# Block transposes and 128-byte DMAs in place of TensorE transposes, a thread per RWKV end, and a pause between narrow visits

## The chip, the core and the metric

The kernel runs on one core of one Trainium2 chip. The metric is the device time of one execution in microseconds (us); several executions are timed and their median is taken. One more execution is profiled. The engines are TensorE (PE; its weight loads PEld), VectorE (DVE), ScalarE (ACT), GpSimd (POOL) and SyncE (SP). SP computes nothing here: it issues DMAs, one after the other, in the order in which the program names them.

## What is computed

One layer of an encoder over 512 frames of 2048 features, in float32. A projection of x feeds two mixers: 16 RWKV-7 heads of 64 and 8 HGRN2 heads of 128. Their gated outputs are concatenated, projected back and added to x ahead of a LayerNorm.

```python
proj = einsum('btd,dc->btc', h, w_in)
rw, hg = token_shift(proj[..., :RWKV_COLS], mu), proj[..., RWKV_COLS:]
# RWKV-7, per frame and head:
S = S * w_t + (S @ a_t) b_t^T + v_t k_t^T ;  o_t = S @ r_t
o = group_norm(o) * gn_w + gn_b + sum(r * k * r_k) * v ;  o_rwkv = o * silu(z)
# HGRN2, chunk by chunk of 64 frames:
o = o_intra + (q * exp(b)) @ S ;  S = S * exp(b_last) + k_dec^T @ i
o_hgrn = o * rsqrt(mean(o*o) + eps) * g_norm_w * silu(z)
h = layer_norm(ALPHA * h + concat(o_rwkv, o_hgrn) @ w_out)
```

## The kernel before, in words

Features lie on the 128 partitions and the 512 frames along them, so a tile is 128x512. Each float32 product of the two large projections is made as three products of reduced-precision halves (`three`, L441): activations `xh`, `xl`, weights `wh`, `wl`. SP loads weights in tiles `wr` of 128x1024 (`load`, L420; two buffers); of each half of a `wr`, a *part*, ACT makes `wh` (L330) and DVE `wl` (`split`, L405; L340). A part feeds 12 main products of 128x128 by 128x512 on TensorE (L446). There are three buffers each of `wh` and `wl`. A `wr` buffer is loaded again once both of its parts are split.

Everything else runs beside these main products, in threads: `rwkv_prep` (one per pair of RWKV heads), `rwkv_invert` and `rwkv_scan` (one per group of two pairs), `rwkv_finish` (the end of a pair), `hgrn_heads` with `hgrn_out` (two heads together, then each head's keys, states and end), and `put_gated`, which stores most gated outputs to HBM until the output projection asks for them. A thread is a generator that yields one instruction or one condition at a time.

`Plan` (L63) writes the program while it is built: it keeps an estimated clock per engine, and after every main product it asks the first thread of each queue (`pump`, L194; `step`, L158) whether its next instruction could start about now. What it takes is written at that place of that engine's queue. So the order of each engine is fixed when the kernel is built; on the chip each engine goes through its own queue in order and waits by semaphores. TensorE's instructions have three modes: *main* (reduced precision, 512 wide), *whole* (f32, 128x128 and all rows) and *narrow* (f32, fewer rows or columns). `TURNS` prices a change of mode, and `worth` (L183) holds a visit back for a moment so that others can join.

Two ways of turning a tile are in the kernel. `tr` (L320) is a TensorE transpose of 128x128 against the identity, into PSUM (L321). `turned` (L385) is the other: DVE transposes each 32x32 block in place in its tile (`dtr`, L358; L359), then 16 DMAs (8 with `rows=2`) on SP's queue carry each row of blocks to its partitions, in pieces of 32 floats, 128 bytes (L394). The planner writes the DMAs in four groups, lets its clock go on by 0.4 us for each DMA of a group, and counts the tile as there 3 us after the last group. Before, `rwkv_prep` turns two tiles per pair so: `bk`, 128x1024, in 16 DMAs, and the values `v` into `zz`, in 8.

The other turns are TensorE's. `rwkv_finish` (L890) transposes four blocks of `o_all` into the PSUM tile `po`, and DVE (L349) multiplies and adds from it into `g`. `hgrn_out` transposes three blocks of keys `k` into `ps`, copied to `kt` (inside the tile `g`) for TensorE's state products, and at its end four blocks of `o2` into `pn`, which DVE multiplies into `g`. All ends of RWKV pairs wait in a single queue, `finishes`, of which only the first thread is asked.

Of the kernel before, what the change touches and what calls it, by code (L numbers as in the profile page):

```python
# [62 lines left out]
class Plan:  # L63
# [8 lines left out]
    TURNS = {("main", "whole"): 0.015, ("whole", "main"): 0.033, ("main", "narrow"): 0.1,  # L72
             ("whole", "narrow"): 0.1, ("narrow", "main"): 0.26, ("narrow", "whole"): 0.2}
    LEAD = -0.35
    SLACK = 0.6
    EARLY = 0.5

    def __init__(self, room):
        self.clock = {"pe": 0.0, "dve": 0.0, "act": 0.0, "pool": 0.0, "dma": 0.0}
        self.table = None  # L80
        self.mode = "main"
# [43 lines left out]
    def issue(self, op, way=None):  # L125
        end, s, r, e, f = way or self.best(op)
        f()
        if e == "pe":
            self.mode = op.mode
        if op.table and self.table not in op.table:  # L130
            self.table = op.table[0]
# [103 lines left out]
def mixer_kernel(ctx, tc, head, x_r, w_all, par, up, ln_wb, consts, hmask, out):  # L235
# [149 lines left out]
    def turned(dst, src, tmp, rows=4, base=0):  # L385
# [5 lines left out]
        for a in range(4):  # L391
            for b in range(rows):
                o = base + 32 * b
                nc.sync.dma_start(dst[o : o + 32, :, 32 * a : 32 * a + 32],  # L394
                                  tmp[32 * a : 32 * a + 32, :, 32 * b : 32 * b + 32])
            at = plan.clock["pe"] + 0.4 * rows
            yield lambda: plan.clock["pe"] >= at
# [492 lines left out]
    def rwkv_finish(S, p):  # L890
# [26 lines left out]
        drop(po)  # L917
        yield stt(z, sz, 1.0, z, ALU.add, ALU.mult)
# [4 lines left out]
    def rwkv_group(SS, grp):  # L923
# [126 lines left out]
    def hgrn_out(S, h, q, k, dt_, dg, tot, tots):  # L1050
# [3 lines left out]
        kt, state = tiles(g)[:, 0:3], tiles(k)[:, 0:3]  # L1054
        yield landed(k)
        ps = take("mix")
        for t in range(3):
            yield tr(ps[:, t * P : t * P + P], k[:, t * P : t * P + P])
        yield copy(kt, tiles(ps)[:, 0:3])
        drop(ps)  # L1060
        yield has(S, "i")
# [26 lines left out]
        S["used"]()  # L1088
        yield landed(o2)
        pn = take("mix")  # L1090
        for j in range(4):
            yield tr(pn[:, j * P : j * P + P], o2[:, j * P : j * P + P])
        yield has(S, "g")
        yield stt(g, pn, hcol(HHW, h), S["g"], ALU.mult, ALU.mult)
        drop(S["g"], pn, o2)
        put_gated(8 + h, g)
# [563 lines left out]
```

## Time and profile before

| | us |
|---|---|
| timed runs, median of 3 | 1053.51 (1051.52 to 1053.82) |
| the profiled execution's own time | 1053.89 |
| its span, first to last instruction | 1052.1 |
| PE busy | 1042.6 (99%) |
| DVE busy | 755.1 (72%) |
| ACT busy | 438.0 (42%) |
| transposes on PE (L321) | 88 |
| DMAs of turned tiles on SP (L394) | 128 of 256 pieces into `q`, 64 into `zz` |
| mean granted TensorE clock | 0.998 |

How to read it: a group of instructions is named by its line, engine, operation, and output<-inputs with the buffer numbers left out. Matmuls overlap, so the step from one start to the next tells more than a length. A f32 matmul that isn't a transpose stands twice in the trace, as two passes. The timeline's columns are start, length, engine and group; the chain of work in order of time has the same without shapes.

### The profile page before, as it was taken

The page shows a single profiled execution, that of the slowest core. Times are in us where ns is not written, and L with a number is a line of the kernel's source. Part 1 is how long each engine was busy: PE and PEld are TensorE (multiplying, and loading weights), DVE is VectorE, ACT ScalarE, POOL GpSimd, SP SyncE. Part 2 cuts the span into 40 slices and gives each one's busy share as a digit, 9 for nine tenths or more (in the row PEclk, how much of TensorE's full clock was granted, in tenths as well). Part 3 has the DMA queues.
Part 4 walks back from the last instruction along what each step waited for, and adds up shares of the span by engine and source line. Part 5 has one row for each costly group of instructions (what it writes and reads, how often), then busy time and mean ns, then how long its engine had stood idle before and what let it go on. Part 6 is the DMA issues. An engine that isn't in the chain of part 4 may idle for free.

```text
span 1052.1 us, 18837 instructions
## 1 busy us (share of the span) xinstructions
PE 1042.6 (99%) x7342; PEld 867.6 (82%) x7342; DVE 755.1 (72%) x1653; ACT 438.0 (42%) x867; POOL 37.4 (4%) x81
## 2 busy tenths in 40 slices
PE   9999999999999999999999999999999999999997
PEld 8888888888888888888888888888888788888885
DVE  7475898667769987676688856865998677725556
ACT  6445243444352344552533344525235454323321
POOL 0000000000000000000000000000000001000000
PEclk9999999999999999999999999999999999999999
DMA  8134343222343522223534223234352143545613
GB/s 332 51 104 113 98 112 86 85 79 80 84 123 101 122 80 85 73 91 80 137 83 123 88 66 100 69 91 122 96 125 70 58 166 126 186 128 158 203 61 130
DMA packets 87305, 114.79 MB, mean 109 GB/s; under 512 B 56368, under 2 KB 58160, under 8 KB 87088
## 3 DMA queue, kind: packets, MB, share of 16 engines
q1 hardware_dynamic: 87072, 113.39, 36.5%
q8 instruction: 58, 0.95, 0.4%
q14 instruction: 31, 0.25, 0.1%
q10 hardware_dynamic: 144, 0.20, 0.1%
HBM read 99.92 MB, written 7.34 MB: 102 GB/s over the span
## 4 chain that ended last, share of the span: by engine, by line
PE 99%; DVE 1%; issue 0%; DVEq 0%
PE main L446 74%; PE mix L317 11%; PE mix L446 8%; PE main L1185 3%; PE main L317 2%; PE mix L321 1%; PE mix L1135 0%; DVE inv L349 0%; DVE inv L340 0%; DVE stats L1542 0%; DVEq L1656 0%; DVE mv L1350 0%; DVE mv L345 0%; DVE inv L1133 0%; DVE mv L349 0%
## 5 line engine op out<-in xcount | busy, mean ns | idle before, releaser
L446 PE MATMUL main<-xh,wl 128*128 128x512 f32 x864 | 342.4, 396 | 0.0
L446 PE MATMUL main<-xh,wh 128*128 128x512 f32 x864 | 341.6, 395 | 0.0
L446 PE MATMUL main<-xl,wh 128*128 128x512 f32 x864 | 340.9, 395 | 0.0
L330 ACT ACTIVATE wh<-wr 128x512 fp32r<-128x512 f32 x299 | 186.8, 626 | 234.9 <-PE main L446 167.2
L340 DVE TENSOR_TENSOR wl<-wr,wh 128x512 fp32r<-128x512 f32 x299 | 203.7, 682 | 61.2 <-ACT wh L330 59.7
L446 PEld LDWEIGHTS main<-xh,wl 128*128 128x128 f32 x864 | 162.7, 188 | 33.0
L446 PEld LDWEIGHTS main<-xl,wh 128*128 128x128 f32 x864 | 162.7, 188 | 32.8
L446 PEld LDWEIGHTS main<-xh,wh 128*128 128x128 f32 x864 | 162.8, 188 | 32.6
L446 PE MATMUL main<-wh,xh 128*128 128x512 f32 (+1 forms) x262 | 102.4, 391 | 0.0
L446 PE MATMUL main<-wh,xl 128*128 128x512 f32 (+1 forms) x262 | 102.1, 390 | 0.0
L446 PE MATMUL main<-wl,xh 128*128 128x512 f32 (+1 forms) x262 | 102.1, 390 | 0.0
L446 PEld LDWEIGHTS main<-wl,xh 128*128 128x128 f32 x262 | 49.2, 188 | 9.8
L446 PEld LDWEIGHTS main<-wh,xl 128*128 128x128 f32 x262 | 49.2, 188 | 9.7
L446 PEld LDWEIGHTS main<-wh,xh 128*128 128x128 f32 x262 | 49.2, 188 | 9.5
L331 ACT ACTIVATE t<-main,om 128x512 f32<-128x512 f32 x33 | 22.4, 687 | 53.5 <-PE main L446 42.3
L349 DVE SCALAR_TENSOR_TENSOR t<-main,pr,t 128x511 f32<-128x511 f32 x33 | 24.4, 747 | 28.1 <-ACT t L331 27.7
L340 DVE TENSOR_TENSOR inv<-inv,inv 64x30 f32<-64x30 f32 (+14 forms) x120 | 38.6, 322 | 2.9
L340 DVE TENSOR_TENSOR inv<-inv 64x30 f32<-64x30 f32 (+14 forms) x120 | 38.4, 320 | 2.3
L340 DVE TENSOR_TENSOR t<-t,tot 128x256 f32<-128x256 f32 x96 | 37.9, 415 | 1.9 <-PE mix L317 1.7
L349 DVE SCALAR_TENSOR_TENSOR bd<-mix,pc,bd 64x64 f32<-64x64 f32 x112 | 31.7, 283 | 9.5 <-PE mix L317 7.2
L330 ACT ACTIVATE zz<-mix 64x64 f32<-64x64 f32 x61 | 13.4, 219 | 45.6 <-PE mix L317 43.9
L331 ACT ACTIVATE t<-main 128x512 f32<-128x512 f32 x32 | 18.5, 598 | 30.6 <-PE main L446 30.2
(222 smaller groups left out, 1331.2 us busy)
## 6 DMA issues: line engine op xcount, KB each, us to landing
wr<-w_all SPq DMA_DIRECT2D x156, 512.0 KB, 3.6
q<-head SPq DMA_DIRECT2D x15, 448.0 KB, 5.5
q<-q SPq DMA_DIRECT2D x128, 32.0 KB, 2.4
g<-x_r SPq DMA_DIRECT2D x16, 256.0 KB, 4.0
spill<-g SPq DMA_DIRECT2D x12, 256.0 KB, 2.8
out<-q SPq DMA_DIRECT2D x12, 256.0 KB, 2.4
t<-spill SPq DMA_DIRECT2D x10, 256.0 KB, 4.0
zz<-ksq SPq DMA_DIRECT2D x64, 32.0 KB, 2.7
```

The lines of the kernel that those rows point to most:

```text
L317: return Op([("pe", cost, lambda: pe.matmul(o, l, r, start=start, stop=stop, **kw))], [l, r], [o], mode="narrow" if narrow else "main" if ...
L321: return Op([("pe", 0.11, lambda: pe.transpose(o, i, ident))], [i], [o])
L330: return "act", cost, lambda: sc_e.activation(o, i, f, scale=scale)
L331: return "act", cost, lambda: sc_e.activation(o, i, f, scale=scale, bias=bias)
L340: return dve_op([a, b], o, lambda: dve.tensor_tensor(o, a, b, f), base=0.16 if o.shape[0] < P and size(o) == C and o.tensor.name in tags e ...
L349: return dve_op([a, b], o, lambda: dve.scalar_tensor_tensor(o, a, s, b, f1, f2), per=0.00113, base=0.085 if o.shape[0] == P else 0.25 if s ...
L446: pe.matmul(ps, l, r, start=first and i == 0, stop=last and i == 2)
L1185: pe.matmul(pss[a], *ops, start=k == 0 and low == of == 0, stop=k == KT - 1 and low == 1)
```

## The change

- Six of the eight RWKV ends (pairs 0 to 5) turn `o_all` by `turned`, through a `ksq` buffer: a block transpose on DVE and 16 DMAs of 32x4x32 on SP. DVE's multiply-add then reads the tile in SBUF itself.
- In HGRN heads 0 to 5 the keys are turned so (16 DMAs of 32x3x32, straight into `kt`), and the end too (16 DMAs of 32x4x32, in place).
- `turned` lets the planner's clock go on by 0.2 us per DMA and not 0.4, for all tiles, `bk` and `zz` too.
- `finishes` becomes two queues, one for each pair of a group.
- After a narrow visit, `worth` lets none begin from another mode for 1.5 us of the planner's clock.

```diff
+    REST = 1.5
...
         if e == "pe":
             self.mode = op.mode
+            if op.mode == "narrow":
+                self.rest = end + self.REST
...
     def worth(self, op, now):
+        if op.mode == "narrow" != self.mode and now < self.rest:
+            return False
...
-            at = plan.clock["pe"] + 0.4 * rows
+            at = plan.clock["pe"] + 0.2 * rows
...
-        drop(sm, sq)
+        drop(sm)
+        if p < 6:
+            yield from turned(o_all, o_all, tiles(sq.rearrange("p a b -> p (a b)")))
+        drop(sq)
...
-        yield landed(o_all)
-        po = take("mix")
-        for j in range(4):
-            yield tr(po[:, j * P : j * P + P], o_all[:, j])
+        if p < 6:
+            po = o_all.rearrange("p j f -> p (j f)")
+        else:
+            yield landed(o_all)
+            po = take("mix")
+            for j in range(4):
+                yield tr(po[:, j * P : j * P + P], o_all[:, j])
...
-                plan.add(finishes, rwkv_finish(S, 2 * grp + i))
+                plan.add(finishes[i], rwkv_finish(S, 2 * grp + i))
...
+        if h < 6:
+            yield room(ksq=1)
+            tmp = take("ksq")
+            yield from turned(kt, tiles(k)[:, 0:3], tiles(tmp)[:, 0:3])
+            drop(tmp)
+        else:
+            yield landed(k)
+            ps = take("mix")
...
+        if h < 6:
+            yield room(ksq=1)
+            tmp = take("ksq")
+            yield from turned(tiles(o2), tiles(o2), tiles(tmp))
+            drop(tmp)
+            pn = o2
+        else:
+            yield landed(o2)
+            pn = take("mix")
...
-    groups, finishes, preps = plan.queue(), plan.queue(), plan.queue()
+    groups, finishes, preps = plan.queue(), [plan.queue(), plan.queue()], plan.queue()
```

The planner writes nearly every queue anew. Rows of the orders below give line, operation, output<-inputs with buffer numbers, shape and count; lines after the change are those of the changed file (L401 there is L394 before, L347 is L340, L356 is L349, L366 is L359, L324 is L317, L453 is L446).

**Place A**, after the scan of the first group. SP before: `q4374` is the `bk` tile of pair 2, `g481` the gated output of pair 0.

```order
L394 DMA q4374_2307<-q4468_2805 32x8x32 x8
L423 DMA wr480_2881<-w_all 128x1024
L394 DMA q4374_2307<-q4468_2805 32x8x32 x8
L423 DMA wr490_2938<-w_all 128x1024
L599 DMA spill_109<-g481_2885 128x512
L423 DMA wr497_2983<-w_all 128x1024
L423 DMA wr507_3029<-w_all 128x1024
L394 DMA zz501_3005<-ksq502_3006 32x8x32 x8
```

SP now: `q4369` is that `bk`, `t141` and `t204` are the ends of pairs 0 and 1.

```order
L401 DMA q4369_2302<-q4482_2931 32x8x32 x16
L430 DMA wr494_3025<-w_all 128x1024
L401 DMA t141_677<-ksq471_2881 32x4x32 x12
L401 DMA t204_1006<-ksq473_2883 32x4x32 x4
L401 DMA t141_677<-ksq471_2881 32x4x32 x4
L401 DMA t204_1006<-ksq473_2883 32x4x32 x8
L430 DMA wr501_3091<-w_all 128x1024
L401 DMA t204_1006<-ksq473_2883 32x4x32 x4
L430 DMA wr510_3140<-w_all 128x1024
L606 DMA spill_109<-g497_3074 128x512
L401 DMA zz512_3150<-ksq513_3151 32x8x32 x8
```

Before, loads stood between the halves of one turn; now three turns, 48 DMAs, stand with two loads among them.

DVE at place A before, from the block transpose of `bk` to the multiply-add of pair 0's end, which reads PSUM (`mix483`):

```order
L359 STREAM_TRANSPOSE q4468_2805<-q4374_2307 128x1024
L340 TENSOR_TENSOR wl472_2828<-wr447_2674,wh471_2827 128x512
L349 SCALAR_TENSOR_TENSOR t475_2841<-main448_2682,pr_104,t475_2841 128x511
L353 TENSOR_REDUCE sm461_2775<-ksq462_2776 128x8
L340 TENSOR_TENSOR wl477_2855<-wr460_2734,wh476_2854 128x512
L346 TENSOR_SCALAR sm461_2775<-sm461_2775 128x8
L340 TENSOR_TENSOR wl479_2877<-wr460_2734,wh478_2876 128x512
L340 TENSOR_TENSOR t141_677<-t141_677,sm461_2775 128x512
L349 SCALAR_TENSOR_TENSOR g481_2885<-mix483_2898,half_106,t106_460 128x512
L340 TENSOR_TENSOR wl485_2913<-wr473_2836,wh484_2912 128x512
```

DVE now, from the block transpose of pair 0's end on; `ksq507` is a half that a TensorE product of pair 3's preparation reads.

```order
L366 STREAM_TRANSPOSE ksq471_2881<-t141_677 128x512
L347 TENSOR_TENSOR t204_1006<-t204_1006,sm472_2882 128x512
L347 TENSOR_TENSOR wl493_3021<-wr481_2919,wh492_3020 128x512
L366 STREAM_TRANSPOSE ksq473_2883<-t204_1006 128x512
L347 TENSOR_TENSOR wl496_3052<-wr488_2975,wh495_3051 128x512
L347 TENSOR_TENSOR wl500_3087<-wr488_2975,wh499_3086 128x512
L356 SCALAR_TENSOR_TENSOR g497_3074<-t141_677,half_106,t106_460 128x512
L356 SCALAR_TENSOR_TENSOR t503_3104<-main487_2972,pr_104,t503_3104 128x511
L356 SCALAR_TENSOR_TENSOR t463_2814<-ksq498_3075,t463_2814 128x512
L347 TENSOR_TENSOR wl505_3115<-wr494_3025,wh504_3114 128x512
L356 SCALAR_TENSOR_TENSOR g497_3074<-g497_3074,half_106,t463_2814 128x512
L347 TENSOR_TENSOR ksq507_3126<-t425_2590,ksq506_3125 128x512
```

The multiply-add `g497<-t141` now reads the tile that the DMAs write, and the splits `wl505` and `ksq507` stand behind it. The block transpose of `bk` (`q4482`) stands five rows ahead of the first of these, with the split `wl486` right behind it.

TensorE at place A before: the four transposes of pair 0's end.

```order
L446 MATMUL main474_2839<-xl26_93,wh476_2854 128x512
L446 MATMUL main474_2839<-xh10_77,wl477_2855 128x512
L321 MATMUL mix483_2898<-cst_100,t141_677 128x128 x4
L446 MATMUL main474_2839<-xh11_78,wh476_2854 128x512
L446 MATMUL main474_2839<-xl27_94,wh476_2854 128x512
```

TensorE now: they are gone; the product that reads `ksq507` stands here, 59 products of 512 columns behind the first one of `wl486`'s part, and `wl505`'s part begins two rows further on.

```order
L453 MATMUL main502_3102<-xh8_75,wh499_3086 128x512
L324 MATMUL mix511_3146<-ksq506_3125,ones_r_102 128x512
L324 MATMUL mix511_3146<-ksq507_3126,ones_r_102 128x512
L453 MATMUL main502_3102<-xl24_91,wh499_3086 128x512
L453 MATMUL main502_3102<-xh8_75,wl500_3087 128x512
L453 MATMUL main502_3102<-xh9_76,wh504_3114 128x512
L453 MATMUL main502_3102<-xl25_92,wh504_3114 128x512
L453 MATMUL main502_3102<-xh9_76,wl505_3115 128x512
```

**Place B**, after the scan of the second group. SP before, around the `bk` of pair 4 (`q4668`):

```order
L394 DMA q4668_4116<-q4811_5022 32x8x32 x8
L423 DMA wr821_5082<-w_all 128x1024
L394 DMA q4668_4116<-q4811_5022 32x8x32 x8
L423 DMA wr831_5141<-w_all 128x1024
L599 DMA spill_109<-g822_5089 128x512
L423 DMA wr838_5184<-w_all 128x1024
L394 DMA zz844_5211<-ksq845_5212 32x8x32 x2
L423 DMA wr848_5232<-w_all 128x1024
L394 DMA zz844_5211<-ksq845_5212 32x8x32 x6
```

SP now: `t428` and `t555` are the ends of pairs 2 and 3, `q4651` and `zz840` pair 4's, `t599` the end of head 3.

```order
L401 DMA t428_2617<-ksq797_5063 32x4x32 x4
L401 DMA t555_3363<-ksq799_5065 32x4x32 x4
L430 DMA wr824_5249<-w_all 128x1024
L401 DMA t555_3363<-ksq799_5065 32x4x32 x4
L401 DMA q4651_4035<-q4820_5207 32x8x32 x16
L430 DMA wr834_5318<-w_all 128x1024
L606 DMA spill_109<-g825_5254 128x512
L401 DMA zz840_5347<-ksq841_5348 32x8x32 x4
L430 DMA wr845_5375<-w_all 128x1024
L401 DMA zz840_5347<-ksq841_5348 32x8x32 x4
L401 DMA t599_3638<-ksq842_5357 32x4x32 x16
L430 DMA wr860_5446<-w_all 128x1024
```

Another 20 DMAs of `t428` and `t555` stand just ahead of these rows, without a load: 72 DMAs of five turns in all. On DVE two block transposes (of `t428`, then of `t555`) and the split `wl819` open this stretch; the multiply-add on `t599` closes it, with the split `wl870` right behind it. On TensorE 118 products of 512 columns and 7 of 128 lie between the first of `wl819`'s part and the one that reads `wl870`.

**Place C**, after the scan of the third group. SP before, around the `bk` of pair 6 (`q41053`):

```order
L394 DMA q41053_6702<-q41147_7200 32x8x32 x8
L423 DMA wr1159_7276<-w_all 128x1024
L394 DMA q41053_6702<-q41147_7200 32x8x32 x8
L423 DMA wr1169_7333<-w_all 128x1024
L599 DMA spill_109<-g1160_7280 128x512
L423 DMA wr1176_7378<-w_all 128x1024
L423 DMA wr1186_7424<-w_all 128x1024
L394 DMA zz1180_7400<-ksq1181_7401 32x8x32 x8
```

SP now: `t794` and `t887` are the ends of pairs 4 and 5.

```order
L401 DMA q41039_6806<-q41157_7488 32x8x32 x16
L430 DMA wr1169_7573<-w_all 128x1024
L401 DMA t794_5018<-ksq1146_7424 32x4x32 x8
L401 DMA t887_5597<-ksq1148_7426 32x4x32 x4
L401 DMA t794_5018<-ksq1146_7424 32x4x32 x4
L401 DMA t887_5597<-ksq1148_7426 32x4x32 x4
L401 DMA t794_5018<-ksq1146_7424 32x4x32 x4
L401 DMA t887_5597<-ksq1148_7426 32x4x32 x8
L430 DMA wr1176_7642<-w_all 128x1024
```

As at place A, three turns stand in a row. DVE has a split (`wl1161`) right behind the block transpose of `q41039`, and behind the multiply-add on `t794` the same six instructions as at place A up to `ksq1182`, which TensorE reads 57 products of 512 columns behind the first of `wl1161`'s part.

More of the change, by code (lines that the diff above doesn't have):

```diff
@@ L80, in __init__ @@
         self.table = None
-        self.mode = "main"
+        self.mode, self.rest = "main", 0.0
         self.queues, self.waiting, self.hurry = [], {}, False
@@ L1054, in hgrn_out @@
         kt, state = tiles(g)[:, 0:3], tiles(k)[:, 0:3]
[L1055 to L1060, printed above, removed]
+        if h < 6:
[6 more added lines that the diff above has]
+            ps = take("mix")
+            for t in range(3):
+                yield tr(ps[:, t * P : t * P + P], k[:, t * P : t * P + P])
+            yield copy(kt, tiles(ps)[:, 0:3])
+            drop(ps)
         yield has(S, "i")
@@ L1088, in hgrn_out @@
         S["used"]()
[L1089 to L1092, printed above, removed]
+        if h < 6:
[7 more added lines that the diff above has]
+            pn = take("mix")
+            for j in range(4):
+                yield tr(pn[:, j * P : j * P + P], o2[:, j * P : j * P + P])
         yield has(S, "g")
         yield stt(g, pn, hcol(HHW, h), S["g"], ALU.mult, ALU.mult)
-        drop(S["g"], pn, o2)
+        if h >= 6:
+            drop(pn)
+        drop(S["g"], o2)
         put_gated(8 + h, g)
```

3 lines of the change are left out of this document (2 added, 1 removed).

## The prediction

> **What bounds the kernel now.** I read the page first: engine shares, then the chain that ended last. All times are in us.
>
> ```profile
> PE 1042.6 (99%) x7342; PEld 867.6 (82%) x7342; DVE 755.1 (72%) x1653; ACT 438.0 (42%) x867; POOL 37.4 (4%) x81
> PE 99%; DVE 1%; issue 0%; DVEq 0%
> PE main L446 74%; PE mix L317 11%; PE mix L446 8%; PE main L1185 3%; PE main L317 2%; PE mix L321 1%; PE mix L1135 0%; DVE inv L349 0%; DVE inv L340 0%; DVE stats L1542 0%; DVEq L1656 0%; DVE mv L1350 0%; DVE mv L345 0%; DVE inv L1133 0%; DVE mv L349 0%
> ```
>
> TensorE is the chain: it has no idle time to give back, so each matmul taken away is time won, and each wait put into its queue is time lost. Next, the chain in order of time and TensorE's timeline, for what one instruction costs there. The reported length of a matmul overlaps the next one; the step from start to start is the price.
>
> ```profile
> 324.64 21.14 PE main L446 x93
> ...
> 207.45 0.39 PE L446 MATMUL main<-xl,wh 128*128 128x512 f32 x1
> 207.68 0.93 PE L321 MATMUL mix<-cst,t 128*128 128x128 f32 x7
> 208.44 0.61 PE L317 MATMUL mix<-zz,q 128*128 128x128 f32 x4
> 208.81 0.48 PE L446 MATMUL main<-xh,wl 128*128 128x512 f32 x1
> 209.13 0.39 PE L446 MATMUL main<-xh,wh 128*128 128x512 f32 x1
> ```
>
> A main product takes 21.14 / 93 = 0.227. Seven transposes take 208.44 - 207.68 = 0.76, so 0.109 each. A visit as a whole costs little more than its instructions: the main product behind it takes 0.32 and not 0.23, but its last instruction takes some 0.03 and not 0.11.
>
> Last, the queue that the change fills: SP's DMA issues, by line and in order of time. The shapes stand in the order shown above: a `q<-q` DMA is 32x8x32, so 256 pieces of 128 bytes; a `wr` load is 128 rows.
>
> ```profile
> L394 SPq DMA_DIRECT2D q<-q x128: 585/608/1749, 75.7 to 769.3; - x128
> DMA to landing us min/median/max: 1.9/2.5/4.9
> L423 SPq DMA_DIRECT2D wr<-w_all x156: 327/328/1347, 16.8 to 991.4; - x156
> ...
> 275.39 0.33 SPq L423 DMA_DIRECT2D wr<-w_all  x1
> 275.81 5.16 SPq L394 DMA_DIRECT2D q<-q  x8
> 281.07 0.55 SPq L423 DMA_DIRECT2D wr<-w_all  x1
> 281.67 5.16 SPq L394 DMA_DIRECT2D q<-q  x8
> ```
>
> SP is busy with one such DMA for 5.16 / 8 = 0.65, gap included, so a turn of 16 takes 10.4 of SP's time whatever the planner writes. The planner counted 0.4 for each before, and counts 0.2 now. Before, that hardly showed: a turned tile was read tens of us later, and two turns never stood back to back.
>
> **The change part by part.**
>
> *Transposes.* They go from 6 x 4 + 6 x 3 + 6 x 4 = 66 places of 88: 66 x 0.109 = 7.2 us, all on TensorE's chain. The order has 110 visits by whole f32 matmuls and not 119; at some 0.02 each that is 0.2.
>
> *Narrow visits.* The pause is meant to join them, but in the order they rise from 30 to 33, since other threads now run at other times. What one costs besides its products:
>
> ```profile
> 157.60 0.39 PE L446 MATMUL main<-wh,xh 128*128 128x512 f32 x1
> 157.92 0.70 PE L317 MATMUL mix<-t 128*32 128x16 f32 x62
> ...
> 158.49 0.70 PE L317 MATMUL mix<-t,t 128*32 128x16 f32 x62
> 159.12 0.50 PE L446 MATMUL main<-wl,xh 128*128 128x512 f32 x1
> 159.45 0.39 PE L446 MATMUL main<-wh,xl 128*128 128x512 f32 x1
> ```
>
> Going in takes 0.32 for 0.23, the first main product afterwards 0.33 for 0.23, and the last group some 0.1 more than the 0.57 of the one ahead (157.92 to 158.49): 0.3 in all, so +0.9 for three more.
>
> *Work of DVE.* Eighteen block transposes come in; 384 columns are estimated by their share of 512.
>
> ```profile
> L359 DVE STREAM_TRANSPOSE ksq<-t x8: 695/698/704, 84.2 to 772.2; 128x512 f32<-128x512 f32 x8
> 276.25 0.68 DVE L353 TENSOR_REDUCE sm<-ksq 128x8 f32<-128x512 f32 x1
> 276.84 0.68 DVE L340 TENSOR_TENSOR wl<-wr,wh 128x512 fp32r<-128x512 f32 x1
> 277.44 0.17 DVE L346 TENSOR_SCALAR sm<-sm 128x8 f32<-128x8 f32 x1
> ```
>
> 12 x 0.70 + 6 x 0.52 = 11.5 us on an engine that is busy for 72%: hidden beside the main products, nothing in the sum. If that cover went it would be 11.5. One 512-wide instruction steps by 0.6 to 0.65 (276.25 to 277.44), which I use below. The multiply-add that read PSUM reads SBUF now: nothing either way.
>
> *What a new DMA costs on SP.* An end's piece is 32x4x32, 128 pieces of 128 bytes; a key's is 32x3x32, 96 of them. No row has these. The nearest from below is the `wr` load, 128 rows in 0.328 + 0.04 gap = 0.37; from above the old turn's 0.65. Issuing time follows the number of pieces in these two rows (128 to 256: 0.33 to 0.61), so I take 0.37 for an end and 0.30 for a key, and keep 0.30 to 0.65 for an end's range. The Trainium skill ("DMA: Bandwidth & Descriptors", Anatomy of one DMA — SWDGE (gpsimd) path, told for the other queue) holds that many descriptors can be emitted before their number costs anything; by that a piece of 128 would cost what one of 256 does, and the sum would be the second rival's. The two rows above disagree.
>
> *Where the wait falls.* DVE takes its queue in order. The end's `g<-t` waits for 16 landings, and behind it on DVE stand the `wl` halves of the weights, for which TensorE's next main products wait. So at each place: time until the landing, plus DVE's work behind it, less the time until TensorE gets to what it wants. That last time starts from the lead of the split ahead of its products:
>
> ```profile
> 288.21 0.68 DVE L340 TENSOR_TENSOR wl<-wr,wh 128x512 fp32r<-128x512 f32 x1
> 291.47 0.39 PE L446 MATMUL main<-xh,wh 128*128 128x512 f32 x1
> ```
>
> This half ends at 288.89, and its first product starts at 291.47: a lead of 2.6, which I let vary by 2 either way.
>
> Place A (ends of pairs 0 and 1, pair 2's `bk`). From the end of the big block transpose SP issues 16 old-sized DMAs (10.4), a load (0.4), then 20 end pieces up to pair 0's last (7.4); that one lands 1.9 after the start of its own issue of 0.4: 19.7. Six DVE instructions follow up to the `ksq` half that TensorE reads next (3.9): 23.6. TensorE gets there after the `wl` behind the block transpose (0.6), the lead (2.6) and 59 main products (13.4): 16.6. The wait is 7.0.
>
> Place C (ends of pairs 4 and 5, pair 6's `bk`). The same with 24 end pieces (8.9): 21.2 + 3.9 = 25.1, against 0.6 + 2.6 + 57 x 0.227 = 16.2. The wait is 8.9.
>
> Place B (ends of pairs 2 and 3, pair 4's `bk` and `zz`, head 3's end). Up to head 3's last piece: 48 small (17.8), 24 old-sized (15.6), four loads and stores (1.5), landing 1.5: 36.4, then two DVE instructions, 37.7. TensorE: a block transpose and a `wl` (1.3), the lead, 118 main products (26.8) and 7 whole f32 matmuls of two passes (1.6): 32.3. The wait is 5.4; loads behind these pieces are as late, and lie beside it.
>
> *The lone turns.* Between a key's first piece and its product the program as written out has 29 to 38 main products, 6.6 or more, with visits about 8; needed are 16 x 0.30 + 0.4 + 1.9 - 0.3 = 6.8. So nothing, from 0 to 4.5 each if a piece cost 0.65. A lone HGRN end needs 7.4 plus a load against 6.6 to 10: up to 1.2 of DVE's time, mostly inside the lead. I put +1 for all, 0 to 6.
>
> Sum: -7.2 - 0.2 + 0.9 + 7.0 + 8.9 + 5.4 + 1.0 = +15.8. The profiled execution took 1053.89 (span 1052.1, 1.8 around it): 1069.7. The median shown is 0.4 lower, so I say **1069**.
>
> **The rivals.**
>
> *All of it hides, faster.* If the multiply-adds of the ends never hold DVE up, only 7.2 + 0.2 - 0.9 = 6.5 stays: 1047. The mechanism is a small issue cost: were a piece of any size issued in the 0.2 that the planner counts, A would need 3.2 + 0.4 + 4.0 + 1.7 + 3.9 = 13.2 against 16.6. It decides at the point where the backlog at A is under 16.6 - 3.9. Against it stand the 0.65 rows, since the 16 old-sized DMAs alone take 10.4. The Trainium skill (same page, Issuing engines are not separate DMA queues) calls the time to initiate a DMA usually small beside the DMA; here it is 0.65 beside 1.9, but sixteen in a row are 10.4. Chance 0.11.
>
> *Pieces cost 0.65 whatever their size.* A gains 20 x 0.28 = 5.6, C 24 x 0.28 = 6.7, B 48 x 0.28 = 13.4; keys stall by 6 x 4.5 = 27, lone ends by some 10 beyond the lead. 1069.7 + 63 = 1132. For it: both old turns have three dimensions like the new ones. Chance 0.06.
>
> *About half the wait.* With pieces at 0.30 and a lead of 4.6, A, B and C shrink by 1.4, 3.4 and 1.7 and by 2.0 each: 8.8 in place of 21.3, so 1057; a little more lead still and gain and loss cancel at 1053. Chance 0.04 for within 0.2%.
>
> **How the numbers follow.** The forecast has 0.79; its own range goes from 1057 (as just worked out) to 1092: pieces at 0.5 add 20, 24 and 48 x 0.13 = 12 and some 6 at the lone turns, a shorter lead 5. With the no-change case the range 1052 to 1092 holds about 8 in 10. Faster by over 0.2% (what a measurement of this kernel can tell): 0.11; within: 0.04; slower: 0.79 + 0.06 = 0.85.
>
> **What would show it.** Right: transposes x22 with 66 fewer steps of 0.109; SP busy without a break for some 20, 35 and 20 us at A, B, C; DVE idle for 6 to 10 us ahead of `g<-t`, ended by a DMA on `t`, and TensorE idle just after, 5 to 9 us each, released by DVE. Issue times of 0.33 and 0.26 for the new pieces. Wrong: TensorE without gaps over 2 us at these places, or issue times near 0.2; or waits of TensorE on `g` itself, at the keys.

## The result, and the profile after

The changed kernel takes 1173.73 us (median of 4 runs, 1172.37 to 1175.36) against 1052.84 for the kernel before, timed beside it: a ratio of 1.1148, 95% interval 1.1131 to 1.1164. So it is slower, as forecast, but by 121 us and not by 16. The profiled execution has a span of 1172.3 (1174.3 in all).

The page after: engine shares, the granted clock in 40 slices, the chain by engine and by line, and the DMA queue.

```profile
PE 1069.6 (91%) x7276; PEld 880.2 (75%) x7276; DVE 763.0 (65%) x1666; ACT 435.9 (37%) x866; POOL 38.4 (3%) x81
...
PEclk9999999989969999989889998899699999999999
...
q1 hardware_dynamic: 125472, 117.73, 35.6%
...
PE 72%; SPq 15%; DVE 5%; DMA 4%; issue 2%; ACT 1%; POOL 0%; DVEq 0%; ACTq 0%
PE main L453 51%; SPq L401 14%; PE mix L324 9%; PE mix L453 7%; PE main L1214 3%; DMA t<-ksq 2%; PE main L324 1%; DMA wr<-w_all 1%; DVE wl L347 1%; DMA g<-ksq 1%; DVE inv L347 1%; SPq L430 1%; DVE t L356 0%; DVE ksq L366 0%; DMA t<-spill 0%
```

TensorE was 99% of the chain. Now SP's issuing of turned DMAs (L401) is 14% of it, some 160 us of the span, while the DMA engines that carry the bytes are no busier than before (35.6% now, 36.5% before). The clock row shows something that the prediction did not have: slices at 8 and 6 tenths, where before all stood at 9 (the mean was 0.998, now it is 0.956).

SP's issues by line, duration in ns as least, median and most. `t<-ksq` are the ends' DMAs, `g<-ksq` the keys', `q` and `zz` the old turns; the last row is the weight load:

```profile
L401 SPq DMA_DIRECT2D t<-ksq x192: 585/599/1803, 222.5 to 843.4; - x192
L401 SPq DMA_DIRECT2D q<-q x128: 585/608/1813, 75.8 to 892.7; - x128
L401 SPq DMA_DIRECT2D g<-ksq x96: 585/597/1550, 195.9 to 765.8; - x96
L401 SPq DMA_DIRECT2D zz<-ksq x64: 585/608/1317, 87.1 to 898.6; - x64
...
L430 SPq DMA_DIRECT2D wr<-w_all x156: 327/328/1034, 16.9 to 1112.1; - x156
```

The 96 pieces of a key's DMA, the 128 of an end's and the 256 of an old turn's are all issued in 0.60 to 0.61 (medians). The forecast had 0.26, 0.33 and 0.61.

Place A and, ahead of it, the keys of head 0, in the timeline: start, length, engine and group, and in brackets the idle time before and what ended it.

```profile
195.91 2.65 SPq L401 DMA_DIRECT2D g<-ksq  x4
198.66 0.53 SPq L430 DMA_DIRECT2D wr<-w_all  x1
199.24 7.64 SPq L401 DMA_DIRECT2D g<-ksq  x12
204.20 0.60 PE L324 MATMUL mix<-bd,q 128*128 128x128 f32 x4
208.49 1.54 PE L324 MATMUL mix<-ia,g 128*128 128x128 f32 x6 [3.69 <-issue]
...
310.37 10.87 SPq L401 DMA_DIRECT2D q<-q  x16
321.34 0.54 SPq L430 DMA_DIRECT2D wr<-w_all  x1
321.99 18.02 SPq L401 DMA_DIRECT2D t<-ksq  x28
336.16 0.63 ACT L338 ACTIVATE ksq<-t 128x512 f32<-128x512 f32 x1 [21.13 <-DMA t<-ksq]
336.70 0.61 ACT L337 ACTIVATE wh<-wr 128x512 fp32r<-128x512 f32 x1
337.34 0.69 DVE L347 TENSOR_TENSOR wl<-wr,wh 128x512 fp32r<-128x512 f32 x1 [21.58 <-ACT wh L337]
337.36 0.79 PE L453 MATMUL main<-xh,wh 128*128 128x512 f32 x1 [14.61 <-ACT wh L337]
337.95 0.63 PE L453 MATMUL main<-xl,wh 128*128 128x512 f32 x1
338.38 0.63 PE L453 MATMUL main<-xh,wl 128*128 128x512 f32 x1
...
340.69 2.52 SPq L401 DMA_DIRECT2D t<-ksq  x4
345.13 0.69 DVE L347 TENSOR_TENSOR ksq<-t,ksq 128x512 fp32r<-128x512 f32 x1 [3.91 <-DMA t<-ksq]
345.88 0.80 PE L324 MATMUL mix<-ksq,ones_r 128*128 128x512 f32 x1 [3.73 <-DVE ksq L347]
```

At the keys, 16 DMAs and a load take SP from 195.91 to 206.88, and the product that reads them starts 1.6 later: TensorE stands for 3.7. At place A SP works without a break from 310 to 340, as forecast. But the first engine held is ACT: an end's tanh goes into a `ksq` buffer from which the turn's DMAs still read. Behind it in ACT's order stands a `wh` half, for which DVE and TensorE wait (14.6). Then DVE waits for the other `ksq` buffer, and TensorE for it (3.7).

At B and C, too, an end's tanh into a `ksq` buffer is held first (ACT stands for 15.9, 12.4 and 22.2), and TensorE stands behind it, twice at B and once at C:

```profile
569.59 0.80 PE L453 MATMUL main<-xh,wh 128*128 128x512 f32 x1 [7.77 <-ACT wh L337]
...
596.19 0.79 PE L324 MATMUL mix<-aah,uph 128*128 128x512 f32 x1 [10.66 <-DVE uph L347]
...
841.39 0.80 PE L453 MATMUL main<-xh,wh 128*128 128x512 f32 x1 [15.64 <-ACT wh L337]
```

After the wait at A the main products step by 0.43 (337.95 to 338.38), not by 0.227. The stretches of the same trace (us; busy time and count of PE, PEld, DVE, ACT, POOL; granted clock; DMA share; GB/s):

```profile
204.00:214.00 10.00, 6.31 (x28) 5.37 (x27) 3.09 (x9) 2.35 (x7) 0.00 (x0) 0.83 0.22 60
...
300.00:322.00 22.00, 22.00 (x114) 18.30 (x113) 14.58 (x26) 4.78 (x8) 3.32 (x3) 1.00 0.31 72
322.00:338.00 16.00, 1.39 (x6) 0.79 (x4) 0.66 (x2) 1.84 (x4) 0.00 (x0) 0.69 0.27 58
...
345.00:352.00 7.00, 6.12 (x15) 4.80 (x16) 3.75 (x7) 0.94 (x2) 0.00 (x0) 0.51 0.54 132
352.00:359.00 7.00, 7.00 (x32) 5.74 (x31) 4.12 (x7) 4.50 (x8) 0.00 (x0) 1.00 0.35 62
```

A stretch of 7 us does 15 matmuls at clock 0.51 and 32 at 1.00. Thirteen stretches at clock 0.5, of 3.4 to 20.5 us, follow TensorE's gaps. Every gap of 2.9 us or more (from start to start) in this trace has one behind it; those of 1.4 to 2.7 bring no new one.

Who waits for turned tiles over the whole span (total, times, longest):

```profile
ACT ksq L338 <- DMA t<-ksq: 71.6, 4, 22.2
...
PE main L453 <- ACT wh L337: 39.4, 4, 15.6
ACT wh L337 <- DMA wr<-w_all: 38.8, 14, 7.5
...
DVE ksq L347 <- DMA t<-ksq: 18.9, 4, 7.1
...
PE mix L324 <- DMA g<-ksq: 15.6, 5, 6.5
DVE g L356 <- DMA t<-ksq: 14.1, 3, 6.6
```

The forecast's own wait, DVE's multiply-add on `t`, is the smallest of these. The reuse of buffers holds longer, TensorE waits for keys directly, and ACT waits 38.8 for late loads, where it waited 21.5 before.

To place the loss I went through TensorE's starts one by one. *Idle* is what steps over 0.6 us have beyond 0.24; *half clock* is the sum of the other steps that begin at clock 0.5; *rest* is what is left of the span.

| kernel | span | idle | half clock | rest |
|---|---|---|---|---|
| before | 1052.1 | 3.9 | 3.4 | 1044.8 |
| after | 1172.3 | 100.5 | 60.6 | 1011.2 |
| no new DMAs, old pace (e5) | 1046.1 | 4.0 | 3.6 | 1038.5 |
| heads alone (e4) | 1127.9 | 60.9 | 43.8 | 1023.2 |
| products ahead of the keys (e9) | 1160.8 | 81.8 | 39.9 | 1039.1 |
| heads, a clock for SP (e10) | 1092.8 | 29.6 | 19.6 | 1043.6 |
| heads, GpSimd (e14) | 1056.8 | 7.8 | 8.9 | 1040.1 |
| heads and pairs 0 and 1, GpSimd (e15) | 1089.4 | 25.8 | 33.0 | 1030.6 |
| ends of heads, GpSimd (e17) | 1046.6 | 2.4 | 0.0 | 1044.2 |

After against before: 96.6 more idle. Of 57.2 us more at half clock, 1 - 0.227 / 0.43 = 47% is lost, 27 (an estimate from the two steps). Less the forecast gain of 6.5 that makes 117 of the 120.2 between the spans.

### The profile page after: what moved, and what is told of

It is laid out like the page before. It is cut to its first block, busy times and chain, and to the rows that moved or that the text cites. A ratio compares the mean times of both kernels' runs of the same rounds, so it can differ in the third digit from the quotient of the medians.

```text
span 1172.3 us, 19162 instructions
## 1 busy us (share of the span) xinstructions
PE 1069.6 (91%) x7276; PEld 880.2 (75%) x7276; DVE 763.0 (65%) x1666; ACT 435.9 (37%) x866; POOL 38.4 (3%) x81
## 3 DMA queue, kind: packets, MB, share of 16 engines
q1 hardware_dynamic: 125472, 117.73, 35.6%
## 4 chain that ended last, share of the span: by engine, by line
PE 72%; SPq 15%; DVE 5%; DMA 4%; issue 2%; ACT 1%; POOL 0%; DVEq 0%; ACTq 0%
PE main L453 51%; SPq L401 14%; PE mix L324 9%; PE mix L453 7%; PE main L1214 3%; DMA t<-ksq 2%; PE main L324 1%; DMA wr<-w_all 1%; DVE wl L347 1%; DMA g<-ksq 1%; DVE inv L347 1%; SPq L430 1%; DVE t L356 0%; DVE ksq L366 0%; DMA t<-spill 0%
## 5 line engine op out<-in xcount | busy, mean ns | idle before, releaser
L453 PE MATMUL main<-xh,wh 128*128 128x512 f32 x864 | 349.6, 405 | 39.4 <-ACT wh L337 39.4
L453 PE MATMUL main<-xl,wh 128*128 128x512 f32 x864 | 348.9, 404 | 0.0
L453 PE MATMUL main<-xh,wl 128*128 128x512 f32 x864 | 348.8, 404 | 0.0
L347 DVE TENSOR_TENSOR wl<-wr,wh 128x512 fp32r<-128x512 f32 x299 | 203.4, 681 | 130.7 <-ACT wh L337 129.2
L453 PEld LDWEIGHTS main<-xh,wh 128*128 128x128 f32 x864 | 167.7, 194 | 75.4 <-ACT wh L337 41.1
L453 PEld LDWEIGHTS main<-xh,wl 128*128 128x128 f32 x864 | 167.7, 194 | 35.4 <-DVE wl L347 1.1
L453 PEld LDWEIGHTS main<-xl,wh 128*128 128x128 f32 x864 | 167.8, 194 | 34.0
L453 PE MATMUL main<-wl,xh 128*128 128x512 f32 (+1 forms) x262 | 103.1, 394 | 0.4 <-DVE wl L347 0.4
L453 PE MATMUL main<-wh,xl 128*128 128x512 f32 (+1 forms) x262 | 102.5, 391 | 0.0
L453 PE MATMUL main<-wh,xh 128*128 128x512 f32 (+1 forms) x262 | 102.0, 389 | 0.0
L453 PEld LDWEIGHTS main<-wl,xh 128*128 128x128 f32 x262 | 49.2, 188 | 11.5 <-DVE wl L347 2.0
L453 PEld LDWEIGHTS main<-wh,xh 128*128 128x128 f32 x262 | 49.2, 188 | 10.1 <-ACT wh L337 0.4
L453 PEld LDWEIGHTS main<-wh,xl 128*128 128x128 f32 x262 | 49.3, 188 | 9.4
L338 ACT ACTIVATE ksq<-t 128x512 f32<-128x512 f32 (+1 forms) x24 | 15.1, 628 | 91.4 <-DMA t<-ksq 71.6
L356 DVE SCALAR_TENSOR_TENSOR bd<-mix,pc,bd 64x64 f32<-64x64 f32 x112 | 31.7, 283 | 19.8 <-PE mix L324 17.9
L347 DVE TENSOR_TENSOR inv<-inv,inv 64x30 f32<-64x30 f32 (+14 forms) x120 | 38.6, 322 | 2.8
L347 DVE TENSOR_TENSOR inv<-inv 64x30 f32<-64x30 f32 (+14 forms) x120 | 38.5, 321 | 2.7
L347 DVE TENSOR_TENSOR t<-t,tot 128x256 f32<-128x256 f32 x96 | 36.8, 417 | 0.9 <-PE mix L324 0.7
L337 ACT ACTIVATE t<-mix 64x128 f32<-64x128 f32 (+2 forms) x64 | 16.3, 270 | 47.9 <-PE mix L324 45.3
```

The source lines that it names most:

```text
L337: return "act", cost, lambda: sc_e.activation(o, i, f, scale=scale)
L338: return "act", cost, lambda: sc_e.activation(o, i, f, scale=scale, bias=bias)
L347: return dve_op([a, b], o, lambda: dve.tensor_tensor(o, a, b, f), base=0.16 if o.shape[0] < P and size(o) == C and o.tensor.name in tags e ...
L356: return dve_op([a, b], o, lambda: dve.scalar_tensor_tensor(o, a, s, b, f1, f2), per=0.00113, base=0.085 if o.shape[0] == P else 0.25 if s ...
L453: pe.matmul(ps, l, r, start=first and i == 0, stop=last and i == 2)
```

## The experiments

**Theory:** all of the loss comes from SP's queue, in which an on-chip DMA costs 0.6, and from a planner that writes the readers ahead of what SP can deliver. **Rivals:** the new order itself costs time; the reuse of `ksq` is the root; the transfers or the form of the pieces are slow; turns by DMA can't gain here at all.

### Without the new DMAs (e1, e5)

```diff
-        yield dtr(tmp, src)
+        if moves:
+            yield dtr(tmp, src)
+        else:
+            yield Op([("dve", 0.07 + size(tmp) * 0.0019, lambda: dve.transpose(dst, src))], [src], [tmp])
...
-            for b in range(rows):
+            for b in range(rows if moves else 0):
```

> The changed kernel without its 288 new DMAs: DVE's block transpose writes straight into the tile that the DMAs would have written, and nothing is carried between partitions, so the blocks stand in wrong places. The queues of TensorE, ScalarE, GpSimd and VectorE keep their order. Theory (SP's issue time of 0.6 for each new DMA, and what waits for those DMAs, make up all of the loss): the forecast's 6.5 us gain is left, 1045 to 1051. Rival (the new order itself is bad, by narrow visits or by threads that crowd each other): over 1060, and gaps of TensorE over 2 us remain away from any DMA.

Measured: 1055.96, ratio 1.0028 (1.0016 to 1.0040). The loss of 121 is gone, so it comes with the 288 DMAs, but the gain did not show: the time lies between the two expected ranges. Around the old turn of pair 2's `bk`, SP and ACT read:

```profile
287.90 11.20 SPq L404 DMA_DIRECT2D q<-q  x16
299.19 7.69 SPq L433 DMA_DIRECT2D wr<-w_all  x3
...
303.31 0.63 ACT L337 ACTIVATE wh<-wr 128x512 fp32r<-128x512 f32 x1 [4.98 <-DMA wr<-w_all]
```

At 0.2 per DMA the planner lets no load in among the 16, and the weights come late. So the second run gave the old turns their 0.4 back, with the same edit besides:

```diff
-            at = plan.clock["pe"] + 0.2 * rows
+            at = plan.clock["pe"] + (0.4 if moves else 0.2) * rows
```

> As the kernel without the new DMAs (nothing is carried between partitions for the ends and keys, so their blocks stand in wrong places), but the old turns of bk and zz are paced by 0.4 us per DMA again. Theory (the faster pace packs 16 old DMAs, some 11 us of SP's queue, ahead of a weight load, and that is why the kernel without new DMAs gained nothing): TensorE's gaps of 1.5 to 2.3 us at 92, 302 and 727 us go, 1046 to 1050. Rival (narrow visits and threads ate the gain): 1053 to 1057 still.

Measured: 1047.85, ratio 0.9949 (0.9936 to 0.9963). That is within the theory's range. Fewer transposes, with pause, queues and block transposes on DVE, bring 5.4 by the ratio; the shorter pace of the old turns alone costs 8.1 (1055.96 - 1047.85).

### Ends and heads apart (e3, e4)

In one run the six heads go back to TensorE (`h < 0`), in the other the six pairs (`p < 0`).

```diff
-        if h < 6:
+        if h < 0:
```

> Only the six RWKV ends are turned by DMAs; keys and ends of the HGRN heads go back to TensorE transposes; pace, threads and pause as changed. Theory: the backlog at the places with two ends and a bk tile stays (gaps of TensorE of 8 to 16 us at each, about 50 in all, and 10 to 15 for the half clock behind them), the waits at the keys go: 1100 to 1120. Rival (the keys, read at once by TensorE, are the main loss): under 1080.

> Only keys and ends of six HGRN heads are turned by DMAs; RWKV ends go back to TensorE transposes. Theory: TensorE waits at each of six keys for 1.5 to 7 us (21 in the changed kernel), some 5 to 10 more at the heads' ends, and runs at half clock for 3 to 7 us after most: 1075 to 1100. Rival (keys and ends of heads are hidden; only the double RWKV ends cost): 1050 to 1058.

Measured: 1116.36, ratio 1.0602 (1.0582 to 1.0623), and 1129.79, ratio 1.0730 (1.0714 to 1.0746). The first came as the theory had it, the second is above both ranges: the heads, for which the prediction had next to nothing, cost more than the pairs.

### Another buffer for tanh (e2)

```diff
-        sz = take("ksq")
...
-        yield act(sz, z, AF.Tanh, scale=0.5)
+        yield act(g, z, AF.Tanh, scale=0.5)
+        yield stt(z, g, 1.0, z, ALU.add, ALU.mult)
```

> The changed kernel, but an RWKV end's tanh goes into its g tile and not into a ksq buffer that the turn's DMAs still read. ScalarE then waits for no DMA there. Theory (SP's issue time is the root; ScalarE's wait is only the first place in which it is felt, and VectorE's multiply-add on the same tile waits as long): 1160 to 1174, waits at the three places with two ends shorter by some 2 us each. Rival (the reuse of the ksq buffer is the main loss, about 71.6 us of ScalarE's waiting): under 1130.

Measured: 1186.94, ratio 1.1264 (1.1238 to 1.1290), slower than the changed kernel: both expectations missed. What the waits name instead:

```profile
DVE ksq L347 <- DMA t<-ksq: 82.7, 5, 26.5
ACT ksq L337 <- DMA t<-ksq: 40.1, 2, 21.9
```

DVE's and ACT's next use of a `ksq` buffer takes over. With this edit another instruction is held first; what it waits for, a turn that isn't done, stays the same.

### What one DMA costs on SP (e7, e13)

```diff
+                if flat:
+                    nc.sync.dma_start(dst[o : o + 32, a], tmp[32 * a : 32 * a + 32, b])
+                    continue
```

> The changed kernel, but each of the 16 DMAs of an RWKV end moves a plain 32x128 block of one column group (32 runs of 512 bytes) and not 32x4x32 (128 runs of 128 bytes), so the blocks stand in wrong places; keys and HGRN ends as changed, as a control in the same run. If the number of runs set SP's time, it would fall well under 0.33 us; if the form with three dimensions set it, it falls to the 0.33 us of a plain load; if a DMA between tiles on the chip costs 0.60 us whatever its form, it stays. The control stays at 0.60. Total by the second case: 1140 to 1165, by the third 1174.

```profile
L402 SPq DMA_DIRECT2D t<-ksq x96: 507/588/596, 320.8 to 837.6; - x96
```

Measured: 0.588 for 32 pieces of 512 bytes, as in the third case; 1166.75 in all (one run), 7 under that case's total. Neither the number of pieces nor three dimensions set SP's time. The next run changes the rows:

```diff
+                if form == 0:
+                    nc.sync.dma_start(dst[:, a, 32 * b : 32 * b + 32], tmp[:, a, 32 * b : 32 * b + 32])
...
+                if form == 2:
+                    nc.sync.dma_start(dst[32 * a + 8 * b : 32 * a + 8 * b + 8], tmp[32 * a + 8 * b : 32 * a + 8 * b + 8])
```

> The changed kernel with the DMAs of the RWKV ends in other forms, 16 per end and 16 KB each as before: pairs 0 and 1 in 128 rows of 128 bytes, pairs 2 and 3 in 64 rows of 256 bytes, pairs 4 and 5 in 8 rows of 2048 bytes. They don't turn the blocks, so the output is not the layer's. The HGRN turns stay as they are, for comparison (0.60 at 32 rows). If SP's time goes by the number of rows that one DMA selects (128 rows of a load took 0.33), the first form takes 0.33 to 0.40 and the last 0.6 or more. If any DMA from the chip's memory to itself costs the same, all three take 0.55 to 0.62. The time stays within 15 of the changed kernel's 1173.7 in the second case and falls by 5 to 25 in the first.

The three forms in order, 128, 64 and 8 rows:

```profile
L402 SPq DMA_DIRECT2D t<-ksq x32: 466/599/607, 319.8 to 340.2; - x32
...
L405 SPq DMA_DIRECT2D t<-ksq x32: 461/594/601, 546.1 to 566.5; - x32
...
L409 SPq DMA_DIRECT2D t<-ksq x32: 624/624/756, 815.5 to 836.8; - x32
```

All three have medians of 0.59 to 0.62; 1165.63 in all (one run). On SP every DMA from the chip's own memory to itself costs about the same here, and the loads with their 0.33 read from HBM. In the changed kernel's trace stores to HBM (`spill<-g`) take 0.38 and a load of only 40 KB (`ksq<-hmask`) 0.43, against 0.61 for an old turn's 32 KB, so it isn't the size either. What is left as the difference between the two rows from which the prediction read a law of pieces is whether HBM is on one side.

### Another queue, a longer pace (e8, e6)

```diff
-                nc.sync.dma_start(dst[o : o + 32, :, 32 * a : 32 * a + 32],
+                q.dma_start(dst[o : o + 32, :, 32 * a : 32 * a + 32],
...
+            yield from turned(kt, tiles(k)[:, 0:3], tiles(tmp)[:, 0:3], q=nc.gpsimd)
```

> The changed kernel with the 288 new DMAs issued by GpSimd and not by SP. Theory (SP's queue is the root): weight loads are no longer late (ScalarE's wait for loads falls to some 20 us from 54), and the places with two ends lose their waits to the extent that GpSimd issues a piece in under 0.6 us; keys keep the turn's own latency. 1090 to 1150 if a piece costs GpSimd as much as SP, over 1174 if it costs 1 us or more. Rival (the transfers themselves crowd the DMA engines): no change from 1174 whichever engine issues.

```profile
L401 POOL DMA_DIRECT2D t<-ksq x192: 548/548/607, 220.8 to 789.1; - x192
...
L401 POOL DMA_DIRECT2D g<-ksq x96: 545/545/716, 196.0 to 722.5; - x96
```

Measured: 1121.20 (one run). The same transfers from another queue give back 52 of the 121, so those 52 aren't the transfers' doing. Not as expected, the loads came hardly sooner: ACT waits 49.5 for them (34.1 by `wh`, 15.4 by `t`) and not 20, against 53.6 in the changed kernel. The old turns still stand on SP, 16 DMAs in a row. The Trainium skill ("DMA: Bandwidth & Descriptors", Issuing engines are not separate DMA queues) says that a second issuer saves no more than the initiating time. The run agrees: the 52 are less than the 173 of issuing (288 x 0.60) that left SP's queue.

```diff
-            at = plan.clock["pe"] + 0.2 * rows
+            at = plan.clock["pe"] + 0.6 * rows
...
-        plan.ready[name] = (plan.clock["pe"] + 3.0, "dma")
+        plan.ready[name] = (plan.clock["pe"] + 3.5, "dma")
```

> The changed kernel with the planner told nearly the truth on one turn: 0.6 us per DMA in place of 0.2, and 3.5 us to the landing in place of 3.0. Theory (the planner reads turned tiles before they can be there): the waits at keys and at lone ends all but go, those with several turns at once stay in part, since each thread still counts SP as its own: 1075 to 1105. Rival (SP has too little time for 288 more DMAs however they are placed): over 1150.

Measured: 1138.78, ratio 1.0811 (1.0790 to 1.0832), between the two expectations, both missed. In the code the pace holds for each turn by itself: two threads that turn at once still write two DMAs per 0.6. That this is what remains isn't shown.

### Does idleness bring the half clock? (e9)

```diff
+            for n in range((14, 26, 11, 3, 15, 3, 0, 0)[h]):
+                pe.matmul(ps, xh[0][:, :P], xh[1], start=True, stop=True)
```

> The changed kernel with 72 more main products on TensorE, whose results are overwritten (14, 26, 11, 3, 15 and 3 of them, 16.3 us at 0.227 each), put right ahead of the state products of HGRN heads 0 to 5, where TensorE stood idle for 4.0, 6.8, 3.4, 1.6, 4.3 and 1.4 us. Nothing else is changed, and no wait ends earlier by it. Theory (idleness itself brings the half clock): the gaps at the keys fill up at no cost, the stretches at clock 0.5 behind them disappear, those behind places A, B and C stay; 1159 to 1168, so 5 to 15 under the changed kernel's 1173.7, although TensorE has 16.3 us more to do. Rival (the half clock has another cause, or is bound to the waits): the stretches behind the keys stay, and the time is 1172 or more, up to 1190 if the gaps are not filled.

The stretch around head 0's keys, 0.83 of the clock and 28 matmuls in the changed kernel:

```profile
204.00:214.00 10.00, 9.72 (x57) 8.22 (x57) 3.67 (x11) 3.13 (x10) 0.00 (x0) 1.00 0.19 57
```

Measured: 1163.24, ratio 1.1045 (1.1028 to 1.1061). With 16.3 us more work the kernel is done 10.5 us sooner, as the theory had it. The stretches at half clock behind the keys at 208.6, 246.1, 488.5 and 720.6 are gone, those behind A, B and C stay. The Trainium skill ("TensorE: Matmul & The Clock Gate", What's actually happening) has the array fall to half rate after an idle window of some 3.4 us and come back after as long a busy one. The stretches here are 3.4 us or multiples of it, which agrees. But gaps of 2.9 already brought them, one of 2.2 did in the kernel before (at 816), and in the trace of e14 (below) stretches of 3.4 stand behind gaps of 1.6 and 1.4 (at 878 and 887) and, at 820, behind a row of small products without a gap over 1.0. So the length of a single gap doesn't settle it.

### A planner that counts the queue (e10, e11, e14, e15)

SP gets a clock; a group is written when it has come up to TensorE's (in e11, with the ends of pairs 0 and 1 besides, up to 1.5 ahead):

```diff
+                plan.sent(0.65)
+            yield lambda: plan.clock["sp"] <= plan.clock["pe"] + 0.3
+        plan.ready[name] = (plan.clock["sp"] + 1.7, "dma")
+        plan.busy[tmp.tensor.name] = (plan.clock["sp"] + 1.7, "dma")
```

> The turns of HGRN heads 0 to 5 alone, with the pause and the two queues, and a planner that keeps a clock for SP: each on-chip DMA counts 0.65 and each load 0.37, a group of a turn is written when SP's clock has come up to TensorE's, and a tile and its temporary count as there and free 1.7 after SP's last DMA. Against the heads alone at 0.2 per DMA (1129.8). Theory (the loss is that the planner writes readers ahead of what SP can deliver): gaps under 12 us in all and no stretch at half clock over 5 us; 42 transposes less are 4.6, so 1046 to 1058. Rival (turns by DMAs cost their time wherever they are written, since SP is one queue): 1080 or more.

> The same planner with SP's clock, its groups written up to 1.5 ahead, and the turns of pairs 0 and 1 as well as those of heads 0 to 5: 50 transposes less, 5.4. Theory: 1046 to 1060, with gaps where pairs 0 and 1 and the next pair's keys and values want SP together. Rival as for the heads alone: 1085 or more.

Measured: 1094.93, ratio 1.0400 (1.0385 to 1.0416), and 1108.93, ratio 1.0527 (1.0509 to 1.0544). Against the heads alone 35 us come back, but as expected by the rival. The loss has moved:

```profile
475.00:840.00 365.00, 363.36 (x2458) 301.10 (x2458) 262.53 (x556) 154.49 (x288) 15.91 (x24) 1.00 0.39 103
840.00:865.00 25.00, 10.12 (x297) 8.15 (x295) 23.88 (x70) 6.69 (x18) 0.00 (x0) 0.70 0.27 72
```

For 365 us TensorE is all but full. Then a scan's small products, with DVE and ACT between them, run without main products to cover them. Old turns of the last pairs, the loads and the new turns share one queue, so that the preparation ends late; that reason is argued. The next two runs take the new turns off that queue, with GpSimd's clock counted at 0.6 each, and give the old turns their 0.4 back:

```diff
+                if own:
+                    plan.clock["pool"] = max(plan.clock["pool"], plan.clock["pe"]) + 0.6
...
+                yield lambda: plan.clock["pool"] <= plan.clock["pe"] + 0.6
...
+            plan.ready[name] = (plan.clock["pool"] + 2.2, "dma")
+            plan.busy[tmp.tensor.name] = (plan.clock["pool"] + 2.2, "dma")
```

> The turns of HGRN heads 0 to 5 alone, issued by GpSimd, which did little; the planner counts 0.6 of GpSimd's clock for each and takes tile and temporary as there and free 2.2 after the last one; old turns stay on SP's queue at 0.4; pause and two queues as changed. Theory (the loss is SP's backlog and readers written ahead of it): no gap ended by a turned tile's DMA, gaps under 12 us in all, 1046 to 1058 with 42 transposes less (4.6). Rival (a turn's delay itself pushes keys and ends to where less covers them): 1070 to 1100, as with a clock for SP (1094.9).

> As the run before, with the ends of pairs 0 and 1 too, 50 transposes less (5.4). Theory: 1045 to 1060. Rival: 1075 to 1110.

Measured: 1059.17, ratio 1.0052 (1.0037 to 1.0067), one us beyond the theory's range, and 1086.42, ratio 1.0304 (1.0287 to 1.0322), as the rival had it. For the heads most of the loss has gone: 1129.8, 1094.9, 1059.2. The last step changes the queue, the planner's count and the old turns' pace together, and how much each brings isn't shown; 1059.2 is still 8 above pause and queues alone (1051.28, below). With the pairs the scan stands uncovered again, although the new turns no longer share SP's queue:

```profile
840.00:865.00 25.00, 9.23 (x265) 7.53 (x267) 22.20 (x70) 7.81 (x23) 0.00 (x0) 0.57 0.13 35
```

That speaks against the shared queue as the whole reason, and the rest of it stays open.

### Pause and queues alone, and fewer turns (e12, e16, e17)

The kernel before with pause and two queues; then, by GpSimd, heads 0 to 3 (the lines shown); then the ends of heads 0 to 5 without their keys.

```diff
-        if h < 6:
+        if h < 4:
```

> The kernel before with the pause of 1.5 after narrow visits and the two queues for the ends alone; old turns at 0.4, no new turns. Theory (pause and queues move order and cost nothing by themselves): 1050 to 1056, the kernel before within 0.3%. Rival (the pause holds work back that TensorE then waits for): 1060 or more.

> The turns by GpSimd with a planner that counts them, for keys and ends of HGRN heads 0 to 3 only: 28 transposes less, 3.1; the last heads, behind which little work is left to cover a delay, stay with TensorE. Theory: pause and queues alone gave 1051.3, so 1047 to 1051, faster than both kernels. Rival (every turn that isn't TensorE's costs more than its 0.76 or 0.44 elsewhere): 1053 to 1060.

> The same for the ends alone of heads 0 to 5, keys by TensorE: 24 transposes less, 2.6. Nothing on TensorE waits for an end soon. Theory: 1048 to 1052. Rival: 1053 to 1060.

Measured: 1051.28, ratio 0.9983 (0.9973 to 0.9992); 1050.59, ratio 0.9971 (0.9960 to 0.9983); 1048.40, ratio 0.9949 (0.9935 to 0.9962); all three within the theory's ranges. Pause and queues cost nothing on balance. Their 2.5 us (1.8 by the ratio) are about what the gap of 2.2 and the 3.4 at half clock behind it were worth, which the kernel before had at 816 in its trace and this one hasn't. The kernel before doesn't fall into that stretch each time: timed beside the last two runs it took 1051.8 to 1052.4 in three executions with a mean clock of 0.999 or 1.000, and 1054.0 to 1054.6 in seven with 0.998. The ends add 2.9 for 24 transposes (2.6 by the step of 0.109; 3.6 by the ratios, each good to some 0.0013): their whole worth, and a kernel 0.5% under the one before. With keys, 28 transposes are worth 3.1 and gave 0.7 (1.3 by the ratios). The page of the last run and its DMAs:

```profile
PE 1038.2 (99%) x7318; PEld 863.6 (83%) x7318; DVE 758.7 (72%) x1654; ACT 438.3 (42%) x872; POOL 93.6 (9%) x177
```

```profile
L401 POOL DMA_DIRECT2D t<-ksq x96: 551/551/828, 206.5 to 670.8; - x96
```

TensorE is back at 99%, and 53 us of issuing lie on an engine that had little else to do.

## Why the prediction was wrong

Slower was right, and so were the places where waits build up. The size, 16 forecast and 121 measured, failed first of all at what one new DMA costs on SP.

- **Transposes and visits (-6.5): right.** The run without new DMAs at the old pace gained 5.4, block transposes on DVE and all; its *rest* is 6.3 shorter.
- **"Issuing time follows the number of pieces", so 0.37 and 0.30: the step that failed.** It is 0.60, with the gap 18.02 / 28 = 0.64. The law was drawn from two rows that differed in more than their pieces: one reads HBM, the other the chip's memory. The Trainium skill's rule that was set aside there ("DMA: Bandwidth & Descriptors", Anatomy of one DMA — SWDGE (gpsimd) path: many descriptors before their number costs anything) holds in these runs for SP's queue too, from 32 to 256 pieces. With 0.65 the prediction's own sum is its second rival's, 1132, which had 0.06.
- **Places A, B, C: the right places, waits too short and begun by another reader.** TensorE stood at A for 14.6 and 3.7 where 7.0 was forecast and 12.6 at the right price; at B for 7.8, 2.1 and 10.7 (5.4, and 18.8); at C for 15.6 (8.9, and 15.6, which agrees by luck, since the path was another). That path: the `ksq` buffers, held until the last piece is read, stop ACT and DVE before the multiply-add does. The sum followed the tile that is written, not the one that is read from.
- **Keys "nothing, from 0 to 4.5 each": wrong.** They stopped TensorE for 4.0, 6.8, 3.4, 1.6, 4.3 and 1.4 from start to start, 21.4 in all; the second rival's 27 was the nearer. Waits at the keys stood among the signs of a wrong prediction.
- **The old turns' shorter pace, costed only where turns meet: 8.1 by itself**, through loads held behind 16 unbroken DMAs.
- **Not in the sum at all: the clock.** Idleness was priced at its own length. At the right price the forecast's idle is 12.6 + 15.6 + 18.8 at the three places, 27 at the keys and 11 at lone ends: 85, against 96.6 measured. To that come 27 at half clock. These two, with the old pace among the first, make up most of the 42 between 1132 and 1173.7; that split is an estimate.
- **The rival "all of it hides"** fell with the price; 1047 is what the change gives when the new DMAs are left out and the old pace is kept (1047.85).

What stays open is why the ends of pairs 0 and 1, by GpSimd's queue and counted, still cost 27 (1086.4 against 1059.2).

## What to carry to other kernels

Price a new instruction from a row that has the same source, destination and queue, and if no such row stands near, take the dearer end: sixteen small DMAs are one long occupation of their queue. A planner has to count that queue as it counts an engine, and hold the temporary until the last DMA has read it. Price a wait of the bound engine with the slow clock behind it, and move first what nobody waits for soon: ends paid in full, keys did not.

## What the runs showed of the hardware

- SP took 0.59 to 0.62 (medians) for an on-chip DMA, with 8 to 128 rows and 32 to 256 pieces; for the weights' loads from HBM 0.33, and 0.53 to 0.54 right behind on-chip ones (the rows at 198.66 and 321.34). GpSimd took 0.55.
- In the changed kernel gaps of 2.9 us and more were followed by 3.4 to 20.5 us at clock 0.5, in which a main product steps by 0.43; one of 2.2 did it in the kernel before, and ones of 1.6 and 1.4 among small products in e14.
